# Three matmuls of 256 columns in place of a pair of 512 and 256, and weights stored 96 bytes into their buffers, in a two-layer decoder trunk

## The chip, the cores and the metric

The kernel runs on one core of a Trainium2 chip. The metric is the device time of one execution in microseconds; the kernel before takes 2139.16 us (median of three runs, 2138.77 to 2139.23). TensorE multiplies, ScalarE and VectorE convert, scale and add, GpSimd does a few small powers, and the transfers of weights are issued from SyncE's queue.

## The reference

A trunk of two layers on 256 tokens of width 2048, in float32. Layer 0 mixes tokens with 16 heads of block attention (one block of 256 keys holds the whole sequence, so it is causal attention), layer 1 with 16 heads of latent attention of low rank; each is followed by an FFN of width 5632 with a causal convolution of width 3 on its gate.

```python
x = x + attention(rms_norm(x, attn_norm[i]))
h = rms_norm(x, ffn_norm[i])
g = conv3(h @ w_gate) + conv_b
x = x + (silu(g) * (h @ w_up)) @ w_down
```

## The kernel before, in words

**Parts.** Every product with a weight matrix is made from parts. A float32 operand is cut into a high part, rounded to the type fp32r, and a low part, the rest; a product is high x high + high x low + low x high. For the weights this is done on the way: SyncE loads a unit of 1 MB into `raw` (L75), four pieces of 128x512 each; for every piece ScalarE writes the high part `whi` (L103) and VectorE the low part `wlo` (L104). Both lie in buffers of 576 columns, 64 more than needed (`ROOM`), and `starts` (L155) says for each unit at which column they begin: its result, in elements of 4 bytes, is the offset. Activations (`h`, `oT`, `a`, `cqT`, `ckvT`) are kept with 256 columns of high part and 256 of low part side by side; `h` begins 8 elements into its buffer (`H_START`, L54).

**Two forms of product.** In the token-major form (`tok_major`, L237) the activation is the stationary operand and the weights stream, 512 columns (288 for one product): six matmuls a piece, L246 to L248 for each half of the tokens. In the feature-major form the weights are stationary, tile by tile (128x128, four to a piece), and the activations stream. `feat_major` (L250) does a tile as a pair: the high weights with all 512 columns of the activation (L272), the low weights with its 256 high ones (L274). The result is then two halves of 256 columns in one accumulator, which `halves` (L290) adds: ScalarE copies one half to `half` (L293), VectorE adds the other (L297), and where there is a residual, that too (L295). `feat_half` (L279) does a tile as three matmuls of 256 columns (L286 to L288), all into the same half of an accumulator, so that nothing is left to add.

**Who uses which.** The pair: gate and up (`plan_gate_up`), down (`plan_down_feat`), and `mla_wq_a`. The triple: both output projections `wo` (`plan_wo`, two output tiles in the halves of one accumulator) and the very last output tile of layer 1. Token-major: the heads' q, k and v of layer 0 (four groups of four heads) and the latent products of layer 1.

**Order.** The order is written out by hand. All pieces form one list of quanta; before each, the pieces some steps ahead are split (`ws.split`), then its matmuls are issued, then what was put to it with `at` or `first`: norms, softmax, transposes, evacuations. There are 1480 quanta: in layer 0 192 for the heads, 64 for wo, 352 for gate and up, 176 for down; in layer 1 104 for the latent products (16 of them for `mla_wq_a`, 32 for `mla_wkv_a`), and again 64, 352 and 176. At the end of each wo stage come the sums of the norm and, four quanta later, two transposes that spread its factor over rows (L371).

**Offsets before.** With the result of `starts` in elements: the heads take 16, 8 and 24 for q, k and v of groups 0 and 1, then 32, 40, 48, 56, 0 and 16. The 16 units of each wo stage take 0, 8, ... 56, two units each. FFN and `mla_wq_a` have 0. Layer 1's latent products have various multiples of 8.

Of the kernel before, what the change touches and what calls it, by code (L numbers as in the profile page):

```python
# [10 lines left out]
F32 = mybir.dt.float32  # L11
# [34 lines left out]

UP_ORDER = ("pairs", "pairs")
DOWN_ORDER = ("pairs", "pairs")
# [66 lines left out]
def trunk(ctx: ExitStack, tc: tile.TileContext, a, out):  # L115
# [39 lines left out]
    def starts(u, j):  # L155

        step = 0
        if u < 48:
            step = HEAD_STARTS[u // 4]
        elif u < 64 or 222 <= u < 238:  # L160
            step = (u - 48) // 2 % 8 if u < 64 else (u - 222) // 2
        elif u == 200:
            step = 2
        elif 201 <= u < 209:
            step = u - 201
        elif 209 <= u < 222:
            step = LATENT_STARTS[u - 209]
        return 8 * step, 8 * step

# [66 lines left out]

    def tok_major(state, lhs, kt, k_last, t_hi, t_lo, n):  # L237

        if kt == 0:
            state["acc"] = [ps_acc.tile([P, 512], F32, name="acc") for _ in range(NT)]  # L240
        src = lhs()
        for t in range(NT):
# [3 lines left out]
            mm(o, hi, t_hi[:, :n], start=kt == 0, stop=False)  # L246
            mm(o, hi, t_lo[:, :n], start=False, stop=False)  # L247
            mm(o, lo, t_hi[:, :n], start=False, stop=kt == k_last)  # L248

    def feat_major(state, rhs, k0, k_last, t_hi, t_lo, n, order="pairs"):  # L250

        if k0 == 0:
            state["acc"] = ps_acc.tile([P, 512], F32, name="acc")
        src, o = rhs(), state["acc"]
        ks = range(n // P)
        steps = {
            "pairs": [(k, part) for k in ks for part in "hl"],  # L260
            "low first": [(k, part) for k in ks for part in "lh"],
            "grouped": [(k, part) for part in "hl" for k in ks],
        }[order]
        for i, (k, part) in enumerate(steps):
            kt = k0 + k
            flags = dict(
                start=k0 == 0 and i == 0, stop=kt == k_last and i == len(steps) - 1,
                skip_group_check=True,
            )
            c = slice(k * P, (k + 1) * P)  # L270
            if part == "h":
                mm(o, t_hi[:, c], src[:, kt, :], **flags)  # L272
            else:
                mm(o[:, :S], t_lo[:, c], src[:, kt, :S], **flags)  # L274

    def open_half(state):
        state["acc"] = ps_acc.tile([P, 512], F32, name="acc")

    def feat_half(state, rhs, k0, k_last, first, t_hi, t_lo, n, half):  # L279

        src = rhs()
        o = state["acc"][:, half * S : (half + 1) * S]
        for k in range(n // P):
            kt = k0 + k
            w_hi, w_lo = t_hi[:, k * P : (k + 1) * P], t_lo[:, k * P : (k + 1) * P]
            mm(o, w_hi, src[:, kt, :S], start=first and k == 0, stop=False, skip_group_check=True)  # L286
            mm(o, w_hi, src[:, kt, S:], start=False, stop=False, skip_group_check=True)  # L287
            mm(o, w_lo, src[:, kt, :S], start=False, stop=kt == k_last, skip_group_check=True)  # L288

    def halves(dst, acc, base=None):  # L290

        t = small.tile([P, S], F32, name="half", bufs=2)
        nc.scalar.copy(t, acc[:, S:])  # L293
# [3 lines left out]
        nc.vector.tensor_tensor(dst, acc[:, :S], t, op=ALU.add)  # L297
        return dst

# [84 lines left out]
    def residual_halves(state, j):  # L384
        halves(xT[:, j, :], state["acc"], xT[:, j, :])

# [229 lines left out]
    for g in range(4):  # L616
        for kind in "qkv":
            state = {}
            for kt in range(KD):
                q = add(tok_major, state, lambda: n1.h, kt, KD - 1)  # L620
# [26 lines left out]
    def plan_wo(norm, order):  # L647
# [7 lines left out]
        for j, kq in order:  # L655
# [5 lines left out]
            def work(t_hi, t_lo, n, j=j, kq=kq, pr=pr, fresh=fresh):  # L661
                if fresh:
                    open_half(states[pr])
                feat_half(states[pr], lambda: env["oT"], 4 * kq, KD - 1, fresh, t_hi, t_lo, n, j % 2)

# [36 lines left out]
    class FTile:  # L702
# [45 lines left out]
    def plan_gate_up(layer, norm):  # L748
        for j in range(NF):
            f = FTile(layer, j, norm)  # L750
            for kind, st in (("g", f.gate), ("u", f.up)):
                for kq in range(4):
                    q = add(lambda t_hi, t_lo, n, st=st, kq=kq: feat_major(
                        st, lambda: norm.h, 4 * kq, KD - 1, t_hi, t_lo, n, UP_ORDER[layer]))
                if kind == "g":
# [15 lines left out]

    def plan_down_feat(norm, layer):
        for j in range(KD):
            st = {}
            tail = norm is None and j == KD - 1
            if tail:
                first(len(quanta), open_half, st)
            for kq in range(NF // 4):
                if tail:
                    q = add(lambda t_hi, t_lo, n, st=st, kq=kq: feat_half(  # L780
                        st, lambda: ffn["a"], 4 * kq, NF - 1, kq == 0, t_hi, t_lo, n, 0))
                else:
                    q = add(lambda t_hi, t_lo, n, st=st, kq=kq: feat_major(
                        st, lambda: ffn["a"], 4 * kq, NF - 1, t_hi, t_lo, n, DOWN_ORDER[layer]))
            if tail:
                at(q, residual, st, j, 0)
            else:
                at(q, residual_halves, st, j)
            if norm is None:
# [7 lines left out]

    plan_down_feat(n3, 0)

# [117 lines left out]
    for r in range(4):  # L917
        state = {}
        for kq in range(4):
            q = add(lambda t_hi, t_lo, n, st=state, kq=kq: feat_major(  # L920
                st, lambda: n3.h, 4 * kq, KD - 1, t_hi, t_lo, n))
            if r == 0 and kq == 0:
# [101 lines left out]

    plan_down_feat(None, 1)

# [123 lines left out]
```

## Time and profile before

| | us |
|---|---|
| median of three runs | 2139.16 |
| the profiled execution | 2138.94 |
| its span | 2137.1 |
| TensorE busy | 2129.4 |
| VectorE busy | 1461.7 |
| ScalarE busy | 1184.6 |

The span is the time from the first to the last instruction that the profiler records. Matmuls are pipelined, so the durations of neighbouring ones overlap and a busy TensorE is not TensorE at its peak; the distance between two starts is what a matmul costs. On the timeline each row gives the start in us, the duration in us, engine, line, operation, output and inputs, sizes, and how many instructions were merged into the row. In a view of stretches each engine's busy time is followed by its number of instructions; the last three columns are TensorE's granted clock, the share of the transfers' engines, and GB/s.

### The profile page before, as it was taken

Reading aid. Unit: us, or ns where it says so; the run is one execution under the profiler, and the core shown is the slowest. Engines: PE = TensorE matmul, PEld = TensorE weight load, DVE = VectorE, ACT = ScalarE, POOL = GpSimd, SP = SyncE. Lnnn points to the kernel's source line nnn. Section 1 sums busy time; section 2 is a strip of 40 time slices with the busy share of each in tenths; the row PEclk is TensorE's granted clock in tenths of the full one; section 3 lists DMA queues with packets and bytes.
Section 4 is the critical chain, followed back from the end, with each engine's and each line's share of the span. In section 5 each row is a group of like instructions: output and inputs, shape, how many; then the busy total and the mean of one; then the engine's idle time right before and its main releaser. Section 6 shows DMA issues by size and latency. Waiting matters only on the chain.

```text
span 2137.1 us, 33882 instructions
## 1 busy us (share of the span) xinstructions
PE 2129.4 (100%) x12439; PEld 1883.5 (88%) x12439; DVE 1461.7 (68%) x3246; ACT 1184.6 (55%) x2418; POOL 45.6 (2%) x37
## 2 busy tenths in 40 slices
PE   9999999999999999999999999999999999999999
PEld 7888889988888888888889889998888888888888
DVE  6766666777777777755556786777777777765554
ACT  6555555555555555545455675555555555554443
POOL 0000000000000000000000110000000000000000
PEclk9999999999999999999999999999999999999999
DMA  7444445455555555555554433555555555555553
GB/s 268 160 175 178 158 158 191 176 186 197 184 191 196 182 194 192 187 195 185 198 188 156 177 132 119 178 178 197 182 193 194 182 196 189 186 202 205 189 203 129
DMA packets 59350, 391.30 MB, mean 183 GB/s; under 512 B 6960, under 2 KB 10032, under 8 KB 13232
## 3 DMA queue, kind: packets, MB, share of 16 engines
q1 hardware_dynamic: 59040, 389.10, 51.6%
q8 instruction: 98, 1.61, 0.3%
q14 instruction: 68, 0.56, 0.1%
q10 hardware_dynamic: 144, 0.04, 0.0%
HBM read 387.01 MB, written 2.10 MB: 182 GB/s over the span
## 4 chain that ended last, share of the span: by engine, by line
PE 97%; DVE 1%; DMA 0%; issue 0%; ACT 0%; POOL 0%; SPq 0%; POOLq 0%; ACTq 0%; DVEq 0%
PE acc L272 45%; PE acc L274 24%; PE acc L247 5%; PE acc L248 5%; PE acc L246 5%; PE acc L286 3%; PE acc L288 3%; PE acc L287 3%; PE sc L511 1%; PE tp L487 1%; PE sc L558 1%; PE tp L547 0%; PE sc L514 0%; DVE wlo L104 0%; PE sc L559 0%; DMA xT<-in_xT 0%
## 5 line engine op out<-in xcount | busy, mean ns | idle before, releaser
L104 DVE TENSOR_TENSOR wlo<-raw,whi 128x512 fp32r<-128x512 f32 (+1 forms) x1480 | 991.1, 683 | 385.9 <-ACT whi L103 382.5
L103 ACT CAST whi<-raw 128x512 fp32r<-128x512 f32 (+1 forms) x1480 | 866.4, 614 | 280.3 <-PE acc L272 173.9
L272 PE MATMUL acc<-h,whi 128*128 128x512 f32 x2880 | 999.2, 390 | 0.0
L274 PE MATMUL acc<-h,wlo 128*128 128x256 f32 x2880 | 812.1, 282 | 0.0
L272 PEld LDWEIGHTS acc<-h,whi 128*128 128x128 f32 x2880 | 540.6, 188 | 113.1
L274 PEld LDWEIGHTS acc<-h,wlo 128*128 128x128 f32 x2880 | 544.3, 189 | 0.0
L272 PE MATMUL acc<-a,whi 128*128 128x512 f32 x1364 | 472.9, 390 | 0.0
L274 PE MATMUL acc<-a,wlo 128*128 128x256 f32 x1364 | 384.6, 282 | 0.0
L272 PEld LDWEIGHTS acc<-a,whi 128*128 128x128 f32 x1364 | 256.0, 188 | 53.7
L274 PEld LDWEIGHTS acc<-a,wlo 128*128 128x128 f32 x1364 | 257.8, 189 | 0.0
L293 ACT COPY half<-acc 128x256 f32<-128x256 f32 x211 | 78.7, 373 | 308.3 <-PE acc L274 308.1
L246 PE MATMUL acc<-whi,h 128*128 128x512 f32 (+1 forms) x448 | 177.1, 395 | 0.0
L247 PE MATMUL acc<-wlo,h 128*128 128x512 f32 (+1 forms) x448 | 171.0, 382 | 0.5 <-DVE wlo L104 0.5
L248 PE MATMUL acc<-whi,h 128*128 128x512 f32 (+1 forms) x448 | 170.1, 380 | 0.0
L286 PE MATMUL acc<-oT,whi 128*128 128x256 f32 x512 | 146.9, 287 | 0.0
L288 PE MATMUL acc<-oT,wlo 128*128 128x256 f32 x512 | 143.8, 281 | 0.0
L287 PE MATMUL acc<-oT,whi 128*128 128x256 f32 x512 | 143.7, 281 | 0.0
L297 DVE TENSOR_TENSOR g<-acc,half 128x256 f32<-128x256 f32 x88 | 37.4, 425 | 121.1 <-ACT half L293 121.1
L247 PEld LDWEIGHTS acc<-wlo,h 128*128 128x128 f32 x448 | 84.4, 188 | 17.2 <-DVE wlo L104 2.1
L248 PEld LDWEIGHTS acc<-whi,h 128*128 128x128 f32 x448 | 84.3, 188 | 16.8
L246 PEld LDWEIGHTS acc<-whi,h 128*128 128x128 f32 x448 | 84.4, 188 | 15.7 <-ACT whi L103 1.2
L286 PEld LDWEIGHTS acc<-oT,whi 128*128 128x128 f32 x512 | 96.7, 189 | 0.2
(153 smaller groups left out, 1594.1 us busy)
## 6 DMA issues: line engine op xcount, KB each, us to landing
raw<-in_ffn_gu SPq DMA_DIRECT2D x176, 1024.0 KB, 4.8
raw<-in_ffn_down SPq DMA_DIRECT2D x88, 1024.0 KB, 4.8
raw<-in_moba_wk SPq DMA_DIRECT2D x16, 1024.0 KB, 4.8
raw<-in_moba_wv SPq DMA_DIRECT2D x16, 1024.0 KB, 4.8
raw<-in_moba_wo SPq DMA_DIRECT2D x16, 1024.0 KB, 4.8
raw<-in_mla_wo SPq DMA_DIRECT2D x16, 1024.0 KB, 4.8
raw<-in_moba_wq SPq DMA_DIRECT2D x13, 1024.0 KB, 4.8
raw<-in_mla_wkv_a SPq DMA_DIRECT2D x8, 576.0 KB, 3.8
```

Of the source, the lines that this page charges most:

```text
L103: self.nc.scalar.copy(hi[:, :n], w)
L104: self.nc.vector.tensor_tensor(lo[:, :n], w, hi[:, :n].bitcast(F32), op=ALU.subtract)
L246: mm(o, hi, t_hi[:, :n], start=kt == 0, stop=False)
L247: mm(o, hi, t_lo[:, :n], start=False, stop=False)
L248: mm(o, lo, t_hi[:, :n], start=False, stop=kt == k_last)
L272: mm(o, t_hi[:, c], src[:, kt, :], **flags)
L274: mm(o[:, :S], t_lo[:, c], src[:, kt, :S], **flags)
L286: mm(o, w_hi, src[:, kt, :S], start=first and k == 0, stop=False, skip_group_check=True)
L287: mm(o, w_hi, src[:, kt, S:], start=False, stop=False, skip_group_check=True)
L288: mm(o, w_lo, src[:, kt, :S], start=False, stop=kt == k_last, skip_group_check=True)
L293: nc.scalar.copy(t, acc[:, S:])
L297: nc.vector.tensor_tensor(dst, acc[:, :S], t, op=ALU.add)
```

## The change

- `feat_major` now is what `feat_half` was: all feature-major products are three matmuls of 256 columns a tile. The pair and `halves` are gone, and with them the buffer `half`; evacuations read 256 columns of the accumulator directly.
- `starts`: 24 elements (96 bytes) for all units, apart from the heads of layer 0 (8 in group 0, 56, 8 and 24 in groups 1 to 3), `mla_wqr` and the latent products after `mla_wkv_a` (8), and `mla_wkv_a` itself (4, 12, ... 60).
- `tok_major` takes `cut`: the heads of groups 1 to 3 are done with `cut` 2, so that each matmul of 512 columns becomes two of 256 with the same stationary operand.

```diff
-HEAD_STARTS = (2, 1, 3, 2, 1, 3, 4, 5, 6, 7, 0, 2)
-LATENT_STARTS = (1, 2, 3, 4, 5, 6, 7, 2, 2, 1, 1, 3, 3)
+HEAD_STARTS = (8, 56, 8, 24)
+HEAD_CUTS = (1, 2, 2, 2)
...
     def starts(u, j):
-        step = 0
+        b = 24
         if u < 48:
-            step = HEAD_STARTS[u // 4]
-        elif u < 64 or 222 <= u < 238:
-            step = (u - 48) // 2 % 8 if u < 64 else (u - 222) // 2
-        elif u == 200:
-            step = 2
+            b = HEAD_STARTS[u // 12]
+        elif u == 200 or 209 <= u < 222:
+            b = 8
         elif 201 <= u < 209:
-            step = u - 201
-        elif 209 <= u < 222:
-            step = LATENT_STARTS[u - 209]
-        return 8 * step, 8 * step
+            b = 8 * (u - 201) + 4
+        return b, b
...
-            o = state["acc"][t][:, :n]
-            mm(o, hi, t_hi[:, :n], start=kt == 0, stop=False)
-            mm(o, hi, t_lo[:, :n], start=False, stop=False)
-            mm(o, lo, t_hi[:, :n], start=False, stop=kt == k_last)
+            for w, x, first, last in ((hi, t_hi, 1, 0), (hi, t_lo, 0, 0), (lo, t_hi, 0, 1)):
+                for c in range(cut):
+                    mm(
+                        state["acc"][t][:, c * m : (c + 1) * m], w, x[:, c * m : (c + 1) * m],
+                        start=kt == 0 and first == 1 and c == 0, stop=kt == k_last and last == 1,
+                        skip_group_check=cut > 1,
+                    )
...
-    def feat_major(state, rhs, k0, k_last, t_hi, t_lo, n, order="pairs"):
...
-    def feat_half(state, rhs, k0, k_last, first, t_hi, t_lo, n, half):
+    def feat_major(state, rhs, k0, k_last, first, t_hi, t_lo, n, half=0):
+        if first and half == 0 and "acc" not in state:
+            open_bank(state)
         src = rhs()
         o = state["acc"][:, half * S : (half + 1) * S]
         for k in range(n // P):
...
             mm(o, w_hi, src[:, kt, S:], start=False, stop=False, skip_group_check=True)
             mm(o, w_lo, src[:, kt, :S], start=False, stop=kt == k_last, skip_group_check=True)
...
-    def halves(dst, acc, base=None):
-        t = small.tile([P, S], F32, name="half", bufs=2)
-        nc.scalar.copy(t, acc[:, S:])
-        if base is not None:
-            nc.vector.tensor_tensor(t, t, base, op=ALU.add)
-        dst = t if dst is None else dst
-        nc.vector.tensor_tensor(dst, acc[:, :S], t, op=ALU.add)
-        return dst
...
-            halves(self.g[:, 2:], self.gate["acc"])
-            nc.vector.tensor_tensor(self.g[:, 2:], self.g[:, 2:], self.norm.rstd_b, op=ALU.mult)
+            nc.vector.tensor_tensor(
+                self.g[:, 2:], self.gate["acc"][:, :S], self.norm.rstd_b, op=ALU.mult
+            )
...
-            u = halves(None, self.up["acc"])
-            nc.vector.tensor_tensor(self.c, self.c, u, op=ALU.mult)
+            nc.vector.tensor_tensor(self.c, self.c, self.up["acc"][:, :S], op=ALU.mult)
...
-                at(q, residual_halves, st, j)
+            at(q, residual, st, j, 0)
...
-        src = halves(None, state["acc"])
+        src = state["acc"][:, :S]
```

More of the change, by code (lines that the diff above doesn't have):

```diff
@@ L241, in tok_major @@
         src = lhs()
+        m = n // cut
         for t in range(NT):
@@ L244, in tok_major, with open_bank @@
             lo = src[:, kt, S + t * P : S + (t + 1) * P]
-            o = state["acc"][t][:, :n]
-            mm(o, hi, t_hi[:, :n], start=kt == 0, stop=False)
-            mm(o, hi, t_lo[:, :n], start=False, stop=False)
-            mm(o, lo, t_hi[:, :n], start=False, stop=kt == k_last)
-    def feat_major(state, rhs, k0, k_last, t_hi, t_lo, n, order="pairs"):
[L255 to L276, printed above, removed]
+            for w, x, first, last in ((hi, t_hi, 1, 0), (hi, t_lo, 0, 0), (lo, t_hi, 0, 1)):
[5 more added lines that the diff above has]
+                    )
+    def open_bank(state):
         state["acc"] = ps_acc.tile([P, 512], F32, name="acc")
-    def feat_half(state, rhs, k0, k_last, first, t_hi, t_lo, n, half):
+    def feat_major(state, rhs, k0, k_last, first, t_hi, t_lo, n, half=0):
+        if first and half == 0 and "acc" not in state:
+            open_bank(state)
         src = rhs()
@@ L382, in residual @@
         )
-    def residual_halves(state, j):
-        halves(xT[:, j, :], state["acc"], xT[:, j, :])
     def store(j):
@@ L619, in trunk @@
             for kt in range(KD):
-                q = add(tok_major, state, lambda: n1.h, kt, KD - 1)
+                q = add(lambda t_hi, t_lo, n, st=state, kt=kt, g=g: tok_major(
+                    st, lambda: n1.h, kt, KD - 1, t_hi, t_lo, n, HEAD_CUTS[g]))
                 if g == 0 and kind == "q" and kt + 1 < KD:
@@ L662, in work @@
                 if fresh:
-                    open_half(states[pr])
-                feat_half(states[pr], lambda: env["oT"], 4 * kq, KD - 1, fresh, t_hi, t_lo, n, j % 2)
+                    open_bank(states[pr])
+                feat_major(states[pr], lambda: env["oT"], 4 * kq, KD - 1, fresh, t_hi, t_lo, n, j % 2)
             last = add(work)
@@ L753, in plan_gate_up @@
                     q = add(lambda t_hi, t_lo, n, st=st, kq=kq: feat_major(
-                        st, lambda: norm.h, 4 * kq, KD - 1, t_hi, t_lo, n, UP_ORDER[layer]))
+                        st, lambda: norm.h, 4 * kq, KD - 1, kq == 0, t_hi, t_lo, n))
                 if kind == "g":
@@ L770, in trunk, with plan_down_feat @@
     n3 = Norm(C_AN + KD, False)
-    def plan_down_feat(norm, layer):
+    def plan_down_feat(norm):
         for j in range(KD):
             st = {}
-            tail = norm is None and j == KD - 1
-            if tail:
-                first(len(quanta), open_half, st)
             for kq in range(NF // 4):
[L779 to L787, printed above, removed]
-                at(q, residual_halves, st, j)
+                q = add(lambda t_hi, t_lo, n, st=st, kq=kq: feat_major(
+                    st, lambda: ffn["a"], 4 * kq, NF - 1, kq == 0, t_hi, t_lo, n))
+            at(q, residual, st, j, 0)
             if norm is None:
@@ L796, in plan_down_feat @@
         return q
-    plan_down_feat(n3, 0)
+    plan_down_feat(n3)
     att2 = ExitStack()
@@ L1023, in trunk @@
     plan_gate_up(1, n4)
-    plan_down_feat(None, 1)
+    plan_down_feat(None)
     assert len(quanta) == len(ws.pieces), (len(quanta), len(ws.pieces))
```

6 lines of the change are left out of this document (2 added, 4 removed).

## The prediction

> **What bounds the kernel now.** The page comes first: span, busy table, clock, chain by engine.
>
> ```profile
> span 2137.1 us, 33882 instructions
> PE 2129.4 (100%) x12439; PEld 1883.5 (88%) x12439; DVE 1461.7 (68%) x3246; ACT 1184.6 (55%) x2418; POOL 45.6 (2%) x37
> PEclk9999999999999999999999999999999999999999
> PE 97%; DVE 1%; DMA 0%; issue 0%; ACT 0%; POOL 0%; SPq 0%; POOLq 0%; ACTq 0%; DVEq 0%
> ```
>
> TensorE is idle for 2137.1 - 2129.4 = 7.7 us of the span, its clock is full throughout, and the chain is 97% TensorE. So the kernel lasts as long as its matmuls take one after another, and every nanosecond between the starts of two neighbouring matmuls counts. The groups by line tell which matmuls:
>
> ```profile
> L272 PE MATMUL acc<-h,whi 128*128 128x512 f32 x2880 | 999.2, 390 | 0.0
> L274 PE MATMUL acc<-h,wlo 128*128 128x256 f32 x2880 | 812.1, 282 | 0.0
> L272 PE MATMUL acc<-a,whi 128*128 128x512 f32 x1364 | 472.9, 390 | 0.0
> L286 PE MATMUL acc<-oT,whi 128*128 128x256 f32 x512 | 146.9, 287 | 0.0
> ```
>
> A "tile" below is one 128x128 block of weights with its two parts. 2880 + 1364 = 4244 tiles are done as a pair (512 columns with the high part, 256 with the low); the 512 tiles of the two wo stages are already three matmuls of 256. The durations in these rows (390 and 282 ns) overlap, so a price must come from starts: the timeline of TensorE, first and last row of an undisturbed stretch, divided by the tiles between.
>
> ```profile
> 1419.99 0.39 PE L272 MATMUL acc<-h,whi 128*128 128x512 f32 x1
> ...
> 1766.66 0.39 PE L272 MATMUL acc<-h,whi 128*128 128x512 f32 x1
> ```
>
> 1000 tiles lie between: 346.67 us, **346.7 ns a tile as a pair**, with a part offset of 0.
>
> **What three of 256 cost.** The kernel before has three stretches that answer: the last output tile of layer 1 (offset 0), and the wo stages, whose offset changes every two units (32 tiles). Each pair of rows is first and last of an undisturbed stretch.
>
> ```profile
> 2117.83 0.28 PE L286 MATMUL acc<-a,whi 128*128 128x256 f32 x1
> ...
> 2132.88 0.28 PE L286 MATMUL acc<-a,whi 128*128 128x256 f32 x1
> ```
> ```profile
> 322.37 0.28 PE L286 MATMUL acc<-oT,whi 128*128 128x256 f32 x1
> ...
> 330.29 0.28 PE L286 MATMUL acc<-oT,whi 128*128 128x256 f32 x1
> ```
> ```profile
> 343.78 0.28 PE L286 MATMUL acc<-oT,whi 128*128 128x256 f32 x1
> ...
> 352.61 0.28 PE L286 MATMUL acc<-oT,whi 128*128 128x256 f32 x1
> ```
> ```profile
> 1344.18 0.28 PE L286 MATMUL acc<-oT,whi 128*128 128x256 f32 x1
> ...
> 1353.70 0.28 PE L286 MATMUL acc<-oT,whi 128*128 128x256 f32 x1
> ```
>
> Offset 0: 15.05 us for 43 tiles, 350.0 ns. Offset 8 elements (32 bytes): 7.92 us for 22, 360.0 ns. Offset 24 (96 bytes), the one that the change uses everywhere: in layer 0 8.83 us for 25 tiles, **353.2 ns**, in layer 1 9.52 us for 28 tiles, **340.0 ns**. The same code, offset, buffers and shape run in two steady rhythms 13 ns apart, each held to the end of its stretch. Against 346.7 one gains 6.7 ns a tile, the other loses 6.5. The whole forecast turns on which of them the FFN falls into.
>
> **The change part by part.** (1) *4244 pairs become triples at offset 24.* At 340.0: 4244 x -6.67 = -28.3 us. At 353.2: +27.7. The tail's 44 tiles go from 350.0 to 340.0 (-0.4) or 353.2 (+0.1). Each tile issues one matmul and one weight load more, which these prices contain, since the triples above issue them too. The bounds are 340.0 and the 360.0 of offset 8; I take 340.0, for a reason given with the first rival.
>
> (2) *The wo stages, 512 tiles, get offset 24 throughout.* What they cost now at mixed offsets:
>
> ```profile
> 399.28 0.40 PE L272 MATMUL acc<-h,whi 128*128 128x512 f32 x1
> ...
> 1343.50 0.28 PE L286 MATMUL acc<-oT,whi 128*128 128x256 f32 x1
> ...
> 1400.12 0.40 PE L272 MATMUL acc<-h,whi 128*128 128x512 f32 x1
> ```
>
> From 322.37 to the end of the stage at 399.28 are 216 tiles, 356.1 ns; from 1343.50 to 1400.12 160 tiles, 353.9 ns. At a mean of 355: -7.7 us at 340.0, -0.9 at 353.2.
>
> (3) *The temporary "half" and its adds go.* Each gate, up, down and wq_a group loses a ScalarE copy and a VectorE add, and reads the accumulator in one step:
>
> ```profile
> L293 ACT COPY half<-acc 128x256 f32<-128x256 f32 x211 | 78.7, 373 | 308.3 <-PE acc L274 308.1
> L297 DVE TENSOR_TENSOR g<-acc,half 128x256 f32<-128x256 f32 x88 | 37.4, 425 | 121.1 <-ACT half L293 121.1
> 405.60:888.20 482.60, 482.60 (x2786) 427.83 (x2785) 358.67 (x696) 276.97 (x568) 0.00 (x0) 1.00 0.54 191
> ```
>
> Some 79 us of ScalarE and as much of VectorE vanish, but in the FFN of layer 0 (the last row: stretch, then busy of TensorE, weight loads, VectorE, ScalarE) VectorE is busy 358.67 and ScalarE 276.97 of 482.60 us, and TensorE has no idle time: worth 0. The same cover carries the faster case: VectorE needs 358.67 us less the adds, TensorE at 340 ns still 473. If that cover were gone the splitting of weights would set the pace; it is far from it. The transfers come at 54% DMA share, the SP queue keeps its order, and 2% faster consumption leaves both in place. No wait is added. At the end nothing changes: the last tile already used the triple and the one-step residual.
>
> (4) *Heads of layer 0.* Here the weights are the 512-column moving operand. Prices from the timeline, offset 8, then 16:
>
> ```profile
> 32.76 0.39 PE L246 MATMUL acc<-whi,h 128*128 128x512 f32 x1
> ...
> 44.32 0.39 PE L246 MATMUL acc<-whi,h 128*128 128x512 f32 x1
> ```
> ```profile
> 281.25 0.40 PE L246 MATMUL acc<-whi,h 128*128 128x512 f32 x1
> ...
> 286.15 0.39 PE L246 MATMUL acc<-whi,h 128*128 128x512 f32 x1
> ```
>
> 11.56 us for 51 matmuls, 226.7 ns, against 4.90 us for 21, 233.3 ns. A piece has six, so 1360 or 1400 ns. Group 0 moves to offset 8: at most 32 of its pieces (q and v) gain 40 ns, I take -0.7 us, since its start waits for transfers. Groups 1 to 3, 144 pieces, get twelve matmuls of 256 with the operands' roles exchanged, which no row shows; the nearest are the triples' 113.3 (340.0/3) to 120.0 (360.0/3), so 1360 to 1440 ns a piece after, against 1360 to 1400 before: -5.8 to +11.5 us. I take 12 x 117.8 = 1413 against 1390 (most stretches are near 1400), +3.3 us, because the offsets chosen include 8, at which the triple was slowest.
>
> (5) *Latent products.* 56 pieces go to offset 8: at most 56 x -40 ns = -2.2, I take -1.9. The 288-wide ones get starts at odd multiples of 16 bytes:
>
> ```profile
> 1161.00:1190.00 29.00, 26.94 (x192) 25.61 (x191) 0.00 (x0) 0.00 (x0) 1.00 0.61 208
> ```
>
> 192 matmuls in some 27 us; a start that no row shows may cost or gain the 3% between the rhythms above: -0.8 to +0.8, taken as 0.
>
> **Sum for the fast rhythm**, against the profiled execution's 2138.94 us (span 2137.1 and 1.8 around it): -28.3 - 0.4 - 7.7 - 0.7 + 3.3 - 1.9 = -35.7, **2103.2**. The median of 2139.16 is 0.2 above that execution: 2103.5. With the bounds of (4) and (5) 2095 to 2112.
>
> **The rivals.** *Slow rhythm in both layers.* Which rhythm a stretch gets is settled where it is entered. The places are these: TensorE breaks its stream for the transposes of the norm's factor, and then runs without any break to the end of the FFN.
>
> ```profile
> 405.36 0.43 PE L371 MATMUL tp<-ident,rstd 128*128 128x128 f32 x2
> 405.54 0.48 PE L272 MATMUL acc<-h,whi 128*128 128x512 f32 x1
> ```
>
> If the stream falls into 353.2 there, it stays: +27.7 + 0.1 - 0.9 + 0.7 for (4) and (5) = +27.6, 2166.8, slower. It decides as soon as more than half the tiles are in that rhythm, since +6.5 and -6.7 nearly cancel. For it: one of two stretches, and it is as steady as the other. Against: the 340.0 rhythm repeats the same three intervals every tile, so nothing seems left in it to collide, while the other one alternates (353, 353, 354); a disturbance can throw a stream from the second into the first more easily than back. That is an argument, not a measurement.
>
> *One layer each.* Layer 0 has 2176 of the tiles, layer 1 2112: the FFN terms cancel within 0.5 us, wo gives -4.3, the rest +0.7, so 2135: hardly to be told from no change. For it: that is just what the two stretches did. Against: both layers enter at the same code.
>
> *The offset does nothing in the FFN*, so that this part of the change is empty: the 13 ns would then belong to the wo stage, and the triple cost what the tail shows, 350.0. 4244 x 3.33 = +14.1, wo -2.6, rest +0.7: 2151. Against: the row at offset 8 is 10 ns off with nothing else changed. The Trainium skill speaks for this rival twice. "TensorE: Matmul & The Clock Gate" (Back-to-back issue gap) gives N/2.4 + 2.5 ns a matmul: one matmul more costs 2.5 ns a tile, an estimate of +10.6 us; the trace agrees in sign and size where the offset is 0 (+3.3 ns). "SBUF — State Buffer" (SBUF: two separate sides) has TensorE never waiting for anyone at its SBUF ports, so that a start address could not matter; the trace disagrees, 340.0 to 360.0 by offset and rhythm.
>
> *A third, worse rhythm* at the 360.0 ns of offset 8: +56.6, +2.6, +0.7: 2199.
>
> **How the numbers follow.** Fast rhythm 0.40, slow in both layers 0.29, one each 0.17, no effect of the offset 0.10, worse 0.04. The prediction is the likeliest, 2103.5, its own range 2095 to 2112. The range has to hold the slow case too, as the two hold most of the chance: 2096 to 2170 leaves out about 0.1. Within 0.2% (4.3 us, about what a measurement can tell) lies most of "one each", 0.12; faster are the fast case and the rest of it, 0.45; slower 0.43.
>
> **What would show it.** On the timeline, the starts of the first matmul of a tile in gate/up and down: 340.0 apart for the fast case, 353 for the slow one, with the three intervals 113, 114, 113 or 117 to 119. The rows for the FFN stretches (482.60 us now) should read 473 or 492. If wo and FFN show different rhythms in one layer, the entry decides, as said. TensorE still without idle time, VectorE down by some 80 us. In groups 1 to 3 of the heads the starts of the 256-wide matmuls should lie 113 to 120 ns apart. Wrong outright would be: TensorE waiting for a split, another granted clock, or a rhythm that changes in mid-stage.

## The result, and the profile after

The changed kernel took **2162.28 us** (median of four runs, 2161.81 to 2162.78) against 2139.01 for the kernel before (2138.77 to 2139.23): ratio 1.0109, interval 1.0091 to 1.0126. It is slower by 23.3 us; the prediction said 2103.5, with 2166.8 as the first rival. Loaded again later, the same program took 2104.9, 2105.0 and 2105.2 (experiments 14 to 16), some 34 us less than the kernel before. Both belong to the result, and most of what follows is about the difference.

The page of the profiled execution, first its span, busy table, clock and chain by engine:

```profile
span 2160.0 us, 43790 instructions
PE 2151.5 (100%) x17547; PEld 2113.6 (98%) x17547; DVE 1389.7 (64%) x3035; ACT 1146.7 (53%) x2207; POOL 45.6 (2%) x37
PEclk9999999999999999999999999999999999999999
PE 98%; DVE 1%; DMA 0%; issue 0%; ACT 0%; POOL 0%; SPq 0%; POOLq 0%; ACTq 0%
```

TensorE is still idle for only 8.5 us (7.7 before), its clock is full, and VectorE has lost 72 us. So the spacing of the matmuls must have grown. TensorE's timeline, the ends of an undisturbed stretch in wo of layer 0, in gate/up of layer 0 and in gate/up of layer 1 (start, duration, then the instruction):

```profile
344.51 0.28 PE L261 MATMUL acc<-oT,whi 128*128 128x256 f32 x1
...
395.51 0.28 PE L261 MATMUL acc<-oT,whi 128*128 128x256 f32 x1
...
412.29 0.28 PE L261 MATMUL acc<-h,whi 128*128 128x256 f32 x1
...
889.29 0.28 PE L261 MATMUL acc<-h,whi 128*128 128x256 f32 x1
...
1424.07 0.28 PE L261 MATMUL acc<-h,whi 128*128 128x256 f32 x1
...
1901.07 0.28 PE L261 MATMUL acc<-h,whi 128*128 128x256 f32 x1
```

51.00 us for 150 tiles of wo are 340.0 ns a tile; 477.00 us for 1350 tiles of gate/up are **353.3**, in both layers alike. Where does the stream change over? At the two transposes, early in gate/up:

```profile
403.23 0.28 PE L262 MATMUL acc<-h,whi 128*128 128x256 f32 x1
403.34 0.28 PE L263 MATMUL acc<-h,wlo 128*128 128x256 f32 x1
403.54 0.43 PE L336 MATMUL tp<-ident,rstd 128*128 128x128 f32 x2
403.73 0.36 PE L261 MATMUL acc<-h,whi 128*128 128x256 f32 x1
403.93 0.28 PE L262 MATMUL acc<-h,whi 128*128 128x256 f32 x1
404.05 0.28 PE L263 MATMUL acc<-h,wlo 128*128 128x256 f32 x1
404.17 0.28 PE L261 MATMUL acc<-h,whi 128*128 128x256 f32 x1
404.29 0.28 PE L262 MATMUL acc<-h,whi 128*128 128x256 f32 x1
```

Up to 403.34 the starts lie 0.11 apart, from 404.05 on 0.12, and so to the end of the FFN. The transposes come 0.20 after their predecessor, not 0.11: they wait for GpSimd's power, which sets the norm's factor. The view of stretches gives the FFN's price (stretch; busy of TensorE, weight loads, VectorE, ScalarE, GpSimd; clock; share of transfers; GB/s):

```profile
403.73:895.65 491.92, 491.92 (x4178) 491.92 (x4178) 329.77 (x610) 260.62 (x482) 0.00 (x0) 1.00 0.53 188
```

491.92 us where the prediction named 473 or 492, with a full clock and VectorE at two thirds.

### The profile page after: what moved, and what is told of

Read it like the earlier page. It is cut to its first block, busy times and chain, and to the rows that moved or that the text cites. A ratio compares the mean times of both kernels' runs of the same rounds, so it can differ in the third digit from the quotient of the medians.

```text
span 2160.0 us, 43790 instructions
## 1 busy us (share of the span) xinstructions
PE 2151.5 (100%) x17547; PEld 2113.6 (98%) x17547; DVE 1389.7 (64%) x3035; ACT 1146.7 (53%) x2207; POOL 45.6 (2%) x37
## 4 chain that ended last, share of the span: by engine, by line
PE 98%; DVE 1%; DMA 0%; issue 0%; ACT 0%; POOL 0%; SPq 0%; POOLq 0%; ACTq 0%
PE acc L261 26%; PE acc L263 26%; PE acc L262 26%; PE acc L242 16%; PE sc L473 1%; PE tp L449 1%; PE sc L520 1%; PE sc L476 0%; PE tp L509 0%; DVE wlo L101 0%; PE sc L521 0%; DMA xT<-in_xT 0%; DVE junk L379 0%; POOL hr L392 0%; ACT whi L100 0%
## 5 line engine op out<-in xcount | busy, mean ns | idle before, releaser
L100 ACT CAST whi<-raw 128x512 fp32r<-128x512 f32 (+1 forms) x1480 | 884.5, 614 | 493.4 <-PE acc L262 400.2
L261 PE MATMUL acc<-h,whi 128*128 128x256 f32 x2880 | 809.5, 281 | 0.0
L262 PE MATMUL acc<-h,whi 128*128 128x256 f32 x2880 | 809.1, 281 | 0.0
L262 PEld LDWEIGHTS acc<-h,whi 128*128 128x128 f32 x2880 | 546.9, 190 | 0.0
L261 PEld LDWEIGHTS acc<-h,whi 128*128 128x128 f32 x2880 | 540.6, 188 | 0.0
L261 PE MATMUL acc<-a,whi 128*128 128x256 f32 x1408 | 395.6, 281 | 0.0
L262 PE MATMUL acc<-a,whi 128*128 128x256 f32 x1408 | 395.6, 281 | 0.0
L242 PE MATMUL acc<-whi,h 128*128 128x256 f32 (+2 forms) x1472 | 283.2, 300 | 0.8 <-ACT whi L100 0.7
L262 PEld LDWEIGHTS acc<-a,whi 128*128 128x128 f32 x1408 | 267.3, 190 | 0.0
L261 PEld LDWEIGHTS acc<-a,whi 128*128 128x128 f32 x1408 | 264.3, 188 | 0.0
L242 PEld LDWEIGHTS acc<-whi,h 128*128 128x128 f32 x1472 | 217.3, 189 | 10.1 <-ACT whi L100 2.0
L242 PE MATMUL acc<-wlo,h 128*128 128x256 f32 (+2 forms) x736 | 171.7, 297 | 0.5 <-DVE wlo L101 0.5
L676 DVE TENSOR_TENSOR g<-acc,rstd_b 128x256 f32<-128x256 f32 x88 | 37.4, 425 | 135.9 <-PE acc L263 133.0
L242 PEld LDWEIGHTS acc<-wlo,h 128*128 128x128 f32 x736 | 118.4, 189 | 5.8 <-DVE wlo L101 1.7
```

The lines of the kernel that those rows point to most:

```text
L100: self.nc.scalar.copy(hi[:, :n], w)
L242: mm(state["acc"][t][:, c * m : (c + 1) * m], w, x[:, c * m : (c + 1) * m], start=kt == 0 and first == 1 and c == 0, stop=kt == k_last and ...
L676: nc.vector.tensor_tensor(self.g[:, 2:], self.gate["acc"][:, :S], self.norm.rstd_b, op=ALU.mult)
```

## The experiments

None of the kernels leaves out work. Where a break is added, it multiplies or transposes the identity (or a part of `h`) into an accumulator that nobody reads. Of the two rhythms, "340" and "353" stand for 340.0 and 353.3 ns a tile. Intervals in ns are differences of the trace's start times, which the timeline rounds to 10 ns.

### 1. A break behind the transposes

```diff
+    def kick():
+        st = ps_tp.tile([P, 512], F32, name="tp")
+        for t in range(NT):
+            mm(st[:, t : t + 1], ident, ones, start=True, stop=True)
...
         at(last + 4, norm.rows)
+        at(last + 6, kick)
```

> The changed kernel with two matmuls of one column (identity by ones, into a bank that nobody reads) two quanta after the norm's factor has been spread, in both layers; the output is not touched. Theory (the rhythm is settled by the break at which a stretch is entered: after one-column matmuls the changed kernel's trace shows 340.0 ns, after the transposes 353.3): both FFNs run at 340.0, some 4260 tiles x -13.3 ns = -56.8 us against the changed kernel's 2162.3, so 2105 to 2107. Rival A (the FFN's own work, that is its moving operand or the evacuations of VectorE and ScalarE, sets 353.3): the stream is back at 353.3 within a few tiles of the break, 2162 to 2163.

2106.34 us, ratio 0.9847 (0.983 to 0.9863): the FFN at 340 in both layers. But the trace does not credit the kick: the stream was already at 340 between the transposes and the kick, by the same code that had left 353 in the changed kernel. The price of the rhythm was right, its cause was not.

### 2. Turning it on purpose

```diff
+                    if j == 15:
+                        at(q, kick)
+                    if j == 30:
+                        at(q, turn_kick)   # two transposes of ident
```

> The changed kernel with two one-column matmuls after the gate of tile 15 and two 128-column transposes of the identity after the gate of tile 30 of both FFNs. Theory: 353.3 ns to tile 15, 340.0 from 15 to 30 (15 x 32 = 480 tiles a layer), 353.3 from there on; 2 x 480 x -13.3 = -12.8 us, 2149 to 2151. Rival A: 353.3 throughout, 2162 to 2163. Rival B (a break of any kind draws a rhythm at random): the two layers, or the two breaks, differ from that pattern.

2149.28 us: the sum fits, the places do not. Layer 0 entered at 340, the kick left it there, and the two transposes turned it to 353. TensorE's timeline around them:

```profile
719.73 0.28 PE L261 MATMUL acc<-h,whi 128*128 128x256 f32 x1
...
729.93 0.28 PE L261 MATMUL acc<-h,whi 128*128 128x256 f32 x1
...
730.27 0.38 PE L352 MATMUL tp<-ident 128*128 128x128 f32 x2
...
731.20 0.28 PE L261 MATMUL acc<-h,whi 128*128 128x256 f32 x1
...
741.79 0.28 PE L261 MATMUL acc<-h,whi 128*128 128x256 f32 x1
```

30 tiles in 10.20 us ahead of them, 340.0; 30 in 10.59 behind them, 353.0. Layer 1 entered at 353 and kept it through both breaks. So the 340 rhythm can be left as well: the first sign against the argument on which the prediction chose it.

### 3 and 4. Other start addresses

```diff
+        if 64 <= u < 152:
+            b = 8 * ((u - 64) // 11)
+        elif 238 <= u < 326:
+            b = 8 * ((u - 238) // 11) + 4
```

The third does this to the changed kernel's gate/up (triples), the fourth to that of the kernel before (pairs), with a kick where the start changes.

> The changed kernel with other starts for the weight parts in gate and up: eight blocks of 11 units (176 tiles), in layer 0 with 0, 32, 64, ... 224 bytes, in layer 1 with 16, 48, ... 240 bytes, each entered through two one-column matmuls; down stays at 96 bytes. Theory (start and entry set the rhythm together): 32 bytes 360.0, 96 bytes 340.0, 0 bytes near 350, and each block steady from its entry. Rival C (the start alone decides nothing beyond the entry): all blocks at 340.0. Rival A: all blocks at 353.3. The starts at odd multiples of 16 bytes are open. Time between 2110 and 2165.

> The kernel before (pairs) with the same sixteen starts in gate and up and the same breaks. If the pair also depends on the start, some block differs from 346.7 ns, and the best one tells whether a pair could beat the triple's 340.0; if the pair has one rhythm whatever the start, all blocks show 346.7 and the time is 2139 to 2141.

2163.41 and 2157.45 us. Mean ns a tile by start in bytes, each at one place and one entry:

| start | 0 | 16 | 32 | 48 | 64 | 80 | 96 | 112 | 128 | 144 to 192 | 208 | 224 | 240 |
|---|---|---|---|---|---|---|---|---|---|---|---|---|---|
| triple | 350.0 | 352.0 | 360.0 | 355.0 | 355.0 | 353.3 | 340.0 | 356.4 | 356.0 | 360.0 | 354.3 | 353.3 | 350.0 |
| pair | 346.7 | 353.3 | 353.3 | 346.7 | 353.3 | 346.7 | 353.3 | 353.3 | 346.7 | 349.3 to 353.3 | 349.3 | 353.3 | 350.0 |

The triple came out as the theory said at 0, 32 and 96 bytes; the pair depends on the start too. No other start of the triple came under 350, and no pair under 346.7. So the spacing goes with the start address, and of these 96 bytes is the one worth having, if it comes out at 340. Whether other starts have a second rhythm too was not tried.

### 5. A series of breaks

```diff
+                if kind == "g" and j:
+                    at(q, brk, "T2", norm)              # two transposes
+                if kind == "u":
+                    at(q, brk, KINDS[(j + 5 * layer) % 11], norm)
```

> In both gate/up stages a break after every 16 tiles: two transposes without a wait after each gate product (from the second on), and after each up product one of eleven breaks in turn (1, 2, 3 or 4 transposes; 2 transposes and 2 one-column matmuls; 2 or 1 one-column matmuls; a plain fp32 matmul of 128 or 64 columns; an fp32r matmul of 128 or 64 columns). Theory A, the kind of break decides: two transposes without a wait always leave 353.3 ns a tile, one-column matmuls always leave what they find, and each other kind has one outcome of its own, the same in its 8 places. Rival B, the moment decides: the same kind leaves 340.0 in some places and 353.3 in others, with no order by kind. Rival C, a break can lead to a spacing other than these two (the 360 or 356 of other offsets). Time: 175 breaks of some 0.2 to 0.6 us each are added, 35 to 105 us, to the 2162 of the changed kernel if all is 353.3, and up to 37 us less if all is 340.0: 2160 to 2270; the answer is in the intervals, not in the total.

2170.21 us. TensorE's timeline, four early breaks of layer 0, the first three with the first matmul behind them (two, two, two, then three transposes):

```profile
415.78 0.38 PE L369 MATMUL tp<-ident 128*128 128x128 f32 x2
415.91 0.37 PE L261 MATMUL acc<-h,whi 128*128 128x256 f32 x1
...
421.46 0.38 PE L369 MATMUL tp<-ident 128*128 128x128 f32 x2
421.60 0.36 PE L261 MATMUL acc<-h,whi 128*128 128x256 f32 x1
...
427.33 0.38 PE L369 MATMUL tp<-ident 128*128 128x128 f32 x2
427.47 0.36 PE L261 MATMUL acc<-h,whi 128*128 128x256 f32 x1
...
433.03 0.49 PE L369 MATMUL tp<-ident 128*128 128x128 f32 x3
```

Between breaks lie 16 tiles: 5.55 us, then 5.73, then 5.56, so the two transposes at 421.46 turned 340 into 353 and those at 427.33 turned it back. They are a switch: of the 86 pairs behind gate products 67 went from 340 to 353 and 17 from 353 to 340, and two left it. Three transposes ended at 340 in 8 of 8 places (seven of them had met 340), a single one-column matmul turned 353 into 340 in 8 of 8, one transpose ended at 353 in 8 of 8 (seven had met 353). So some kinds showed one outcome, as theory A says, though most of them met one rhythm nearly always and are hardly tried from the other. The pair of transposes, of which theory A was sure, has both outcomes, and one-column matmuls do not leave what they find.

### 6. The heads without halves

```diff
-HEAD_STARTS = (8, 56, 8, 24)
-HEAD_CUTS = (1, 2, 2, 2)
+HEAD_STARTS = (8, 8, 8, 8)
+HEAD_CUTS = (1, 1, 1, 1)
```

(on the kernel of experiment 1)

> The kernel of e1 (one-column matmuls early in the FFN) with the heads of layer 0 all in 512-column products at an offset of 8 elements, no halves. Theory: the heads cost by their spacing alone; the first three groups of the changed kernel took 299.8 us at 1.3 us more than before, and at 226.7 ns a matmul all twelve parts cost 1536 pieces... of 6 matmuls x 226.7 ns = 1.360 us, so heads of 192 pieces 261.2 us plus the attention's own matmuls as they are: 3 to 5 us less than in e1, 2101 to 2103 if the FFN stays at 340.0. Rival: the halves cost nothing, heads unchanged, 2106. Second question: the edit lies ahead of the FFN and moves nothing in it; if the FFN's rhythm hangs on a few ns of the restart, it may come out at 353.3 in one or both layers, some 28 us each, 2130 or 2158.

2100.95 us, five runs at 2100.5 to 2101.0 and one at 2129.13, which is the profiled one: FFN at 340 in layer 0, at 353 in layer 1. Two results. The heads, first row here, second the changed kernel of experiment 14 (stretch, TensorE, weight loads, VectorE, ScalarE):

```profile
5.52:300.72 295.20, 294.78 (x1365) 243.91 (x1365) 204.50 (x611) 166.42 (x344) 16.90 (x9) 1.00 0.52 188
```
```profile
5.63:305.62 299.99, 299.57 (x2228) 284.62 (x2229) 204.78 (x611) 167.26 (x345) 16.89 (x9) 1.00 0.51 185
```

The halves, with the offsets that came with them, cost 4.8 us. And one program gave two rhythms in two executions: what decides differs from one execution to the next.

### 7. Transposes that wait for nothing

```diff
-        at(last + 4, norm.rows)
+        at(last + 5, norm.rows)
...
-                    at(q, f.evac_gate)
+                    at(q + (1 if j == 0 else 0), f.evac_gate)
```

> The changed kernel with the two transposes that spread the norm's row, and the eviction of the first gate product that needs them, one piece later in both layers, so that TensorE doesn't wait for GpSimd's pow there (85 to 90 ns before). Theory: transposes in a running stream turn it to 353.3 as in the second experiment, so both layers stay at 353.3 and the time is 2162 as for the changed kernel. Rival: the stop of TensorE ahead of the transposes is what turns the stream; without it the 340.0 of wo is kept through the FFN and the time is 2105 to 2107; one layer each, 2134.

2133.89 us in a narrow band (2133.09 to 2134.35, eight runs): 353 in layer 0, 340 in layer 1. The timeline's ends of a stretch behind the transposes in each:

```profile
406.32 0.28 PE L261 MATMUL acc<-h,whi 128*128 128x256 f32 x1
...
419.04 0.28 PE L261 MATMUL acc<-h,whi 128*128 128x256 f32 x1
...
1418.21 0.28 PE L261 MATMUL acc<-h,whi 128*128 128x256 f32 x1
...
1433.85 0.28 PE L261 MATMUL acc<-h,whi 128*128 128x256 f32 x1
```

36 tiles in 12.72 us, 353.3; 46 in 15.64, 340.0. This is the third case that the expectation names, one layer each; neither the theory nor the rival holds for both. Without the wait the outcome did not differ among these eight runs, but it still differs by place. (The transposes come one quantum behind the norm's sums, `last + 3` and `last + 4`, not four; here two.)

### 8 and 10. A third transpose

```diff
+        nc.tensor.transpose(pb[:, NT * P : (NT + 1) * P], ident, ident)
```

(behind the loop in `spread_rows`; the tenth has the whole heads too)

> The changed kernel with one more transpose (of the identity, into an unread part of the same PSUM tile) behind the two that spread the norm's row, in both layers: 0.11 us each. Theory: the kind of break sets the rhythm; in the series three transposes left 340.0 in 8 of 8 places, from either rhythm, so the FFN runs at 340.0 in both layers: 2162.3 - 56 = 2106 to 2107. Rival: the restart after the wait for GpSimd decides and a third transpose changes nothing but the moment: 353.3 in one or both layers, 2134 or 2162.

> The third transpose of e8 and whole heads together, nothing else. Theory: 5.4 us less than e8, as the heads gave between e1 and e6: 2100.5 to 2101.5 in every run. Rival: the restart's few ns decide, since the heads ahead of it shift the moment: 2129 or 2157 in some runs or in all.

The rival, in both. Experiment 8: 2162.31 us (six of nine runs at 2162 to 2163, three at 2134), ratio 1.0066 (1.0029 to 1.0103). Experiment 10: 2156.86 (four of six at 2157, one at 2128.55, one at 2100.23). Three transposes in a running stream had led to 340; behind a wait they lead mostly to 353. Timeline of experiment 8:

```profile
403.48 0.28 PE L263 MATMUL acc<-h,wlo 128*128 128x256 f32 x1
403.68 0.43 PE L336 MATMUL tp<-ident,rstd 128*128 128x128 f32 x2
403.95 0.27 PE L339 MATMUL tp<-ident 128*128 128x128 f32 x1
...
404.77 0.28 PE L261 MATMUL acc<-h,whi 128*128 128x256 f32 x1
...
422.44 0.28 PE L261 MATMUL acc<-h,whi 128*128 128x256 f32 x1
```

50 tiles in 17.67 us, 353.4. The outcome goes with the moment of the restart instead. Over all profiled executions with this entry (experiments 3, 4 and 7 have another), the interval from the last matmul to the waiting transposes was 201 to 206 ns:

| transposes | interval, ns | restarts | led to 340 | led to 353 |
|---|---|---|---|---|
| two | 205 or 206 | 18 | 18 | 0 |
| two | 201 to 204 | 6 | 2 | 4 |
| three | 206 | 5 | 0 | 5 |
| three | 203 | 1 | 1 | 0 |

The rows were cut after the outcomes were known, and three transposes have one restart at 203 alone: the table shows that the two go together, not that the interval is the cause.

### 9 and 12. Mending it behind the restart

```diff
+    def hold():
+        st = ps_tp.tile([P, 512], F32, name="tp")
+        mm(st[:, :1], ident, ones, start=True, stop=True)
...
+                if kind == "u" and j in (0, 1):
+                    at(q, hold)
```

The ninth is the changed kernel with whole heads and holds at 0, 1, 2, 5, 10, 20 and 43; the twelfth is experiment 10, the one that came out badly, with the two holds shown.

> The changed kernel with whole heads (offset 8, no halves) and one one-column matmul behind the up products of tiles 0, 1, 2, 5, 10, 20 and 43 of both layers, no other break. Theory: a one-column matmul turns 353.3 into 340.0 (8 of 8 places in the series) and leaves 340.0 as it is, so whatever the spread transposes leave, it is mended within the first tiles (11 us a tile; at most 0.5 us lost a layer): 2100.5 to 2102.5 in every run, where the sixth experiment had one run at 2129. Rival: a one-column matmul turns the rhythm both ways, as two transposes do; then some of the stretches run at 353.3 and the time lies between 2110 and 2145.

> The kernel of e10 (third transpose, whole heads), which came out at 353.3 in one or both layers in 5 of 6 runs, with one one-column matmul behind the up products of tiles 0 and 1 of both layers. Theory: the one-column matmul mends 353.3: the profile shows up to 32 tiles at 353.3 after the transposes and then 340.0, and the time is 2100.3 + 4 x 0.2 + at most 0.9 = 2101 to 2102 in every run. Rival: from the rhythm that the waiting transposes leave, a one-column matmul in a running stream leads back to 353.3 (as in layer 1 of the second experiment): 2129 or 2158 in some or all runs.

Experiment 9: 2104.24 us, all four runs within 1.1 us, but 3.3 more than experiment 6 and above the 2100.5 to 2102.5 expected: in the trace each of the 14 one-column matmuls costs 0.25 us (start to start across it, less the undisturbed spacing). Both its layers had entered at 340, so nothing was mended in the profiled execution. Experiment 12: **2101.52 us** (2101.2 to 2102.7, five runs), ratio 0.9826 (0.9813 to 0.9839), with two holds a layer the cheaper form of it. In its layer 0 the three transposes did leave 353, and the mending can be read off:

```profile
398.99 0.28 PE L261 MATMUL acc<-h,whi 128*128 128x256 f32 x1
...
403.94 0.28 PE L261 MATMUL acc<-h,whi 128*128 128x256 f32 x1
...
404.29 0.28 PE L347 MATMUL tp<-ones,ident 128*128 128x1 f32 x2
404.43 0.36 PE L261 MATMUL acc<-h,whi 128*128 128x256 f32 x1
...
404.86 0.28 PE L261 MATMUL acc<-h,whi 128*128 128x256 f32 x1
...
409.96 0.28 PE L261 MATMUL acc<-h,whi 128*128 128x256 f32 x1
```

14 tiles in 4.95 us, 353.6 (353.4 from the unrounded starts), then 15 in 5.10, 340.0. Layer 1 had entered at 340. So the mending behind a restart is seen at one place; for the rest it rests on the five even times, against experiment 10 in another loading.

### 11. Breaks of growing length

```diff
+        mm(st[:, :n], norm.h[:, 0, :P], norm.h[:, 1, :n], start=True, stop=True)
```

(behind every product, n = 68, 72, ... 412)

> In both gate/up stages one fp32r matmul of n columns behind every product (16 tiles), n = 68, 72, 76, ... 412, the same series in both layers: a break that adds from some 28 to 172 ns and moves the moment of the restart in steps of 4 columns (1.67 ns). Theory: the rhythm that was there and the moment of the restart against a fixed cycle decide, so the outcome by n and rhythm before is the same in both layers, and runs in bands: several neighbouring n give the same, and the bands come back with a period of n (8 cycles are 8 columns, 32 are 32). Rival A: an fp32r matmul always leaves 340.0, whatever its length (6 of 8 places in the series with 64 columns). Rival B: no order, neighbouring n and the two layers differ at random. Time: 174 breaks of 0.1 us on average, 17 us, on 2106 to 2162: 2123 to 2180.

2143.82 us. Rhythm of the 87 stretches in order, F for 340 and S for 353:

```
layer 0  FFFFFFFFFFFFSFFFSFSSFSFFSSFSFFFSFFSFSFFSFFFSFFFSSFSFSSFFFSSSSSSFFFSFSSFSFFFFSSFSFFSFFFS
layer 1  FFFFFFFFFFFFSFFFSFSSFSFFSSFSFFFSFFSFSFFSFFFSFFFSSFSFSSFFFSSSSSSFFFSFSSFSFFFFSSFSFFSFFFS
```

All 87 agree: the theory's repetition, without its bands. Both layers entered at an interval of 206 ns and met the same breaks, none of which waits, and there the outcome was no chance. The first eleven lengths all ended at 340; behind them no bands by n appeared, so a fixed period is not shown. Either rhythm can be left: in each layer, of 54 breaks that met 340, 22 ended at 353; of 32 that met 353, 21 ended at 340.

### 13 to 17. The changed kernel again, and with holds alone

The thirteenth and seventeenth add the two holds of experiment 12 to the changed kernel and nothing else; the others are the changed kernel itself.

> The changed kernel with one one-column matmul behind the up products of tiles 0 and 1 of both layers, and nothing else. Theory: the changed kernel is 2162.3 only because both FFNs run at 353.3; the mended stream saves 2 x 2112 tiles x 13.33 ns = 56.3 us less up to 0.9 us until the mending and 0.8 us of breaks: 2106.0 to 2107.5 in every run. Rival: the fast time of the other kernels hangs on another of their edits, not on the rhythm alone: above 2130 in some runs or all.

> The changed kernel once more, unaltered, on the same chip. Theory A: its rhythm is drawn anew in each execution, at the restart behind the spread transposes, as in e6 and e8: 2162 in most runs, but 2134 or 2106 in some. Rival B: it is fixed by the program, as the first four runs at 2162 and the four of e1 at 2106 suggest: 2162 in all.

> The changed kernel unaltered, on whatever chip it falls. Theory A: the rhythm behind the spread transposes is drawn with the few ns of the restart, which hang on the chip, the loading of the program or the single execution: 2105, 2134 or 2162, the same in most runs of one loading. Rival B: 2105 is the rule and the first four runs at 2162 were the exception of one chip: 2105 in all.

> The same program as in e15, loaded once more on the same chip. If the chip decides, the time is that of e15; if the loading or the execution decides, it may be another of 2105, 2134 and 2162.

> The kernel of e13 (one-column matmuls behind two products of each FFN) on the same chip: 2106 to 2107.5 in every run, whatever e15 and e16 show; where the spread transposes leave 353.3, its trace shows the turn to 340.0 at the one-column matmul. Rival: 2134 or 2162 in runs where the changed kernel has them.

With holds 2106.42 (2105.87 to 2106.97) and 2106.01 us; in both traces, as in those of the unaltered kernel in these loadings, both layers had entered at 340 already, so these two runs do not test the mending. The unaltered kernel 2104.91 us (five runs within 1.2 us, ratio 0.9842, 0.9828 to 0.9855), 2105.01 and 2105.24 (four runs each). The page of experiment 14, its FFN of layer 0, and its timeline at the restart and across gate/up:

```profile
span 2103.3 us, 43790 instructions
```
```profile
403.74:877.12 473.38, 473.38 (x4178) 473.38 (x4178) 329.55 (x610) 254.56 (x482) 0.00 (x0) 1.00 0.54 195
```
```profile
403.35 0.28 PE L263 MATMUL acc<-h,wlo 128*128 128x256 f32 x1
403.56 0.43 PE L336 MATMUL tp<-ident,rstd 128*128 128x128 f32 x2
...
412.00 0.28 PE L261 MATMUL acc<-h,whi 128*128 128x256 f32 x1
...
871.00 0.28 PE L261 MATMUL acc<-h,whi 128*128 128x256 f32 x1
```

As many matmuls as at first, and 459.00 us for the 1350 tiles that took 477.00, 340.0 each. The transposes start 206 ns behind their predecessor, at first 202 (0.21 and 0.20 in the rows). GpSimd's power ahead of them, first of the execution at 2160.0, then of this one:

```profile
402.42 1.07 POOL L330 TENSOR_TENSOR rstd<-ms,mhalf 128x2 f32<-128x2 f32 x1 [114.87 <-DVE ms L328]
```
```profile
402.42 1.08 POOL L330 TENSOR_TENSOR rstd<-ms,mhalf 128x2 f32<-128x2 f32 x1 [114.88 <-DVE ms L328]
```

In ns it ended 4 later against the sums that feed it. In the 3 us ahead of the restart TensorE's own starts keep the same distances within 1 ns in the two traces, and the other engines' starts move by up to 3 ns against them; 28 us a layer go with that. That this shift alone does it was not tried by itself. Rival B of experiment 14 (fixed by the program) is out, and so is theory A's 2162 in most runs. Experiments 15 and 16 came out as rival B of experiment 15 has it, 2105 in all, which does not tell a rare draw from an exception. The chip is not separated either: experiment 14 ran on one, 15 and 16 on another, and where the first result ran is not on record; but in experiments 6, 8 and 10 the outcome differed between executions on one chip. Why most runs of one loading agree while loadings differ stays open; so does how often 2162 comes up: 4 of 17 runs here, all of one loading.

## Why the prediction went as it did

The sum by stages, from first starts in the traces, against the kernel before, in us:

| term | for 340 | experiment 14 | for 353 | first profile |
|---|---|---|---|---|
| FFN, `mla_wq_a`, tail | -28.7 | -28.7 | +27.8 | +28.0 |
| wo | -7.7 | -6.7 | -0.9 | -6.7 |
| heads, with their start | +2.6 | +2.1 | +2.6 | +2.1 |
| latent products | -1.9 | -0.5 | -1.9 | -0.5 |
| all | -35.7 | -33.8 | +27.6 | +22.9 |

- *What bounds the kernel* held in every run: TensorE has no idle time to win or lose, so spacing decides. *The removed adds* were worth 0, as said: VectorE lost 72 us and ScalarE 38 (some 79 had been named for each), and TensorE's idle time did not move.
- *The price of both rhythms* was right to 0.3 us over 4288 tiles, and so was the place: the transposes at the start of each FFN, then no change to its end.
- **The step that failed** is the one by which the likeliest case was chosen: "a disturbance can throw a stream from the second into the first more easily than back". The break at that place is two transposes, and for these it is false: in experiment 5 they turned 340 into 353 in 67 of 68 places and 353 into 340 in 17 of 18. (Several other kinds of break did lead to 340 more often than away from it, but none of them stands there.) At the place itself the transposes wait for GpSimd, and the outcome goes with a few ns of that wait (28 of 30 restarts in the table are told apart by it); what in those ns decides stays open. Nothing in the profile of before could show which; it showed one stretch of each, and an even chance for the two, with a range to both ends, was all that it supported. The range held the time. That later loadings came within 2 us of 2103.5 is the same draw falling the other way, and no support for the argument.
- *wo* was forecast at 353 for the slow case, as if one draw served a whole layer. It came out at 340 in every kernel with the change. wo is entered from attention, the FFN through the transposes: two entries, two draws. That is -5.8 us of the -4.7 by which the sum for 353 was off (+27.6 against +22.9); the other terms make +1.1.
- *One layer each*, 2135, is what experiment 7 measured at 2133.9.
- *The offset does nothing*: refuted by the triple's 340.0 to 360.0 in experiment 3. By the Trainium skill, "TensorE: Matmul & The Clock Gate" (Back-to-back issue gap), the gap of an isolated matmul of 256 columns is 256/2.4 + 2.5, some 109 ns, and no address enters it; for a stream the section counts the weight loads too, which the prediction's 2.5 ns leaves out. The runs gave 113.3 (340.0/3) at best and 117.8 or 120.0 else. And "SBUF — State Buffer" (SBUF: two separate sides) has TensorE waiting for nobody at its ports; a start address that moves the same stream by 6% does not fit that, though what lengthens it was not found.
- *Heads*: predicted +3.3 for the halves, from a choice near the middle of -5.8 to +11.5; with the gain at group 0 the sign and the size were right. Experiment 6 shows that the other choice, whole products at 8 elements, would have been 4.8 better than the halves, and so some 2.7 under the kernel before.

## What to carry to other kernels

Where a stream of matmuls runs without idle time, read the distance between starts, not the durations, and read it on both sides of every break: a stream can have several steady spacings by start address, and keep for hundreds of us the one at which it was restarted. If a break that waits for another engine stands ahead of a long stretch, one measured time may be a draw; load the program several times before believing it. A cheap break in the running stream (here a one-column matmul of 0.25 us) can put it back, but its effect has to be measured at its place.

## What the runs showed of the hardware

- One program, two steady rhythms 4% apart on the same operands (340.0 and 353.3 ns a tile at 96 bytes), kept over 2112 tiles: in one profiled execution it restarted at 353 in layer 0, 202 ns behind the last matmul, in another at 340, 206 ns behind it. Where no break waits for another engine the choice repeated exactly: 87 of 87 stretches in experiment 11.
- Two transposes toggle it (84 of 86), three in a running stream ended at 340 (8 of 8, seven of them at 340 before), three behind a wait mostly at 353 (5 of 6 profiled restarts). A single one-column matmul turned 353 to 340 in 9 of 9 places, but a pair of them is no sure cure: it did so in 7 of 7 places of experiment 5, yet left layer 1 of experiments 2 and 6 at 353, and the norm's sums left `mla_wq_a` there in the changed kernel's first trace and in experiments 7, 8 and 10.
- What happens inside is open. Spacings by start run from 340.0 to 360.0 ns for triples and from 346.7 to 353.3 for pairs, and no rule for them was found; operand reads against weight loads is a guess that no run here tested.
